# Grouped-query attention: two heads' values in two column groups, as one block at a set place of an explicit TensorE order

## The chip, the cores and the metric

The kernel runs on one core of one Trainium2 chip. The metric is the time of one execution in device microseconds; lower is better. The core has five engines that run side by side: TensorE (PE, its weight loads shown as PEld), VectorE (DVE), ScalarE (ACT), GpSimd (POOL) and SyncE (SP, which here mostly issues transfers), and 16 DMA engines.

## The reference

Two layers of a trunk with two parallel attentions. The change is in branch B, grouped-query attention: 8 query heads of 64 channels share 2 key/value heads. 512 latent tokens look at 768 keys (256 context and 512 latent); in the first layer the 256 context tokens also look at the 256 context keys. All is float32.

```python
def _attend(q, k, v):
    s = jnp.einsum('bqkgd,btkd->bkgqt', q, k).astype(jnp.float32) * (HEAD_DIM ** -0.5)
    p = jax.nn.softmax(s, axis=-1).astype(v.dtype)
    return jnp.einsum('bkgqt,btkd->bqkgd', p, v)

def _merge(a_att, b_att, a_z, b_z, g_a, g_b, w_o_a, w_o_b, w_out):
    o_a = (a_att * jax.nn.silu(a_z)) @ w_o_a
    o_b = (b_att * jax.nn.silu(b_z)) @ w_o_b
    merged = jax.nn.sigmoid(g_a) * o_a + jax.nn.sigmoid(g_b) * o_b
    return merged @ w_out
```

x is 512 x 1024, w_in 1024 x 5376, w_o_a and w_o_b 512 x 1024, w_out 1024 x 1024.

## The kernel before

Each layer projects its input with w_in, runs the neighbourhood attention (branch A), projects branch B's keys, values and queries, runs the grouped-query attention, and then does B's output projection, the merge and the last projection. Float32 accuracy comes from splitting: a projection operand is a high and a low part, and each product is three matmuls (mm3, lines 424 to 426). Probabilities and values are split into two float16 halves each.

**One head of the grouped-query attention, before.** gq_first stages the head's queries (stage_q, lines 872 and 873), all 512 or 768 columns at once. gq_scores goes through four tiles of 128 queries: the scores are four matmuls into one of two PSUM buffers called s (lines 879 and 880); DVE takes the row's maximum (1153); ACT takes the exponential and its sum (1154); turned makes the two float16 halves, the high one by ACT (830), the low one by DVE or, for tiles 1 and 3, by POOL (831); and SP issues a transposing DMA into ht (835). In the first layer ctx_scores does the same for the context queries. gq_values then makes the head's result from ht: divide turns the reciprocal sums by four TensorE transposes (842) and multiplies the gate zb by them (843); then 12 matmuls of 512 columns (1170, 1171) give a PSUM tile whose upper and lower 64 rows belong to the two halves of V; head_out copies one half by ACT (817), adds the other by DVE (818) and lets POOL multiply zb by it (822). ctx_values does the same for the context queries with four matmuls (917).

**Filling.** While DVE, ACT, POOL and the DMAs work on a head, TensorE gets pieces of other projections from a list called fill: the branch gates' columns of w_in that are left (g_chunks, evicted by ACT, 614) and then branch A's output projection (o_chunks, evicted by DVE, 696). One list item is the load of a chunk's weights, or a piece of one feature block and one span of tokens (512 or 256 columns), 24 matmuls for a gate piece and 12 for an output piece; one item, prepare, splits branch A's result into high and low parts (660 by ACT, 661 by POOL). In this stage every piece takes the one PSUM bank called f. The first layer has 40 items left at the first head and the second 24. pipeline runs over the heads: scores of head h, values of head h - 1, then an eighth of the items.

**Order.** The program's order is only a priority: at compile time the framework's scheduler puts each engine's instructions in the order in which it expects them to become ready, and that order is then fixed. behind(engine, fn, after) ties the instructions that fn adds on one engine into a chain behind the named ones; latest(engine, n) names the last n. Before, nothing in the grouped-query attention was tied. Buffers also order: p tiles (NP_GQ, two in the first layer), h tiles (NH_GQ), two ht tiles.

ada_gate finishes the residual gate's modulation: a few DVE instructions, one TensorE transpose (309), an ACT copy, a DMA. In the first layer it stood at the end of the background steps bg, before the attention.

Of the kernel before, what the change touches and what calls it, by code (L numbers as in the profile page):

```python
# [28 lines left out]
NP_GQ = (2, 4)  # L29
# [6 lines left out]
SPLIT_POOL = (1, 3)  # L36
GATES = (3, 3)
PRE_NA, PRE_GQ = 1, 2
ON_PE, ON_DVE = mybir.EngineType.PE, mybir.EngineType.DVE
# [22 lines left out]
def hybrid_kernel(es: ExitStack, tc, x, ctx, cvec, w_ada, w_ada0, small, gvec, w_in, w_o_a, w_o_b, w_out,  # L62
# [521 lines left out]
    def layer(l, hx, nxt, start):  # L584
# [8 lines left out]
        def gate_steps(halves, pool):  # L593
            return (ada_steps(l, range(16, 24), halves, nv, pool)
                    + ([lambda: ada_gate(l, nv, pool)] if 1 in halves else []))
# [128 lines left out]
        else:  # L724
# [5 lines left out]
            bg = gate_steps((0, 1), hp["p"])  # L730
# [49 lines left out]
        if True:  # L780
# [29 lines left out]
            def head_out(po, e, dst, eng=None, back=None):  # L810
# [5 lines left out]
                if back is None:  # L816
                    S.copy(a, po[o:o + 64, :n])
                    V.tensor_tensor(a, po[m:m + 64, :n], a, ALU.add)
                else:
                    S.activation(a, po[o:o + 64, :n], AF.Copy, scale=back[o:o + 64])  # L820
                    V.scalar_tensor_tensor(a, po[m:m + 64, :n], back[m:m + 64], a, ALU.mult, ALU.add)
                (eng or G).tensor_tensor(dst, dst, a, ALU.mult)
# [14 lines left out]
            def divide(ps, r, e, dst, back):  # L837

                n = r.shape[-1]
                V.reciprocal(r, r)  # L840
                for i in range(n):
                    T.transpose(ps[:, 128 * i:128 * i + 128], r[:, i:i + 1].to_broadcast([128, 128]), ident)
                V.scalar_tensor_tensor(dst, ps[64 * e:64 * e + 64, :128 * n], back[64 * e:64 * e + 64], dst,
                                       ALU.mult, ALU.mult)
# [22 lines left out]
            def stage_q(src, e):  # L867

                n = 768 if first else 512
                qs = att["p"].tile([128, n], F32R, tag=f"qs{e}", name=nm("qs"), bufs=1)  # L870
                q = rows(src, e)[:, :n]
# [13 lines left out]
            def ctx_scores(q, kh, kl, ct, late=True):  # L885

                pss = ps_score()
                for i in range(2):
                    scores(pss, q[:, 512 + 128 * i:640 + 128 * i], kh, kl,
                           [(256 * i, 256, cut(512, 768))])  # L890
                mx = sp.tile([128, 2], F32, tag="mx", name=nm("mx"), bufs=8)
                p = p_tile()
                if late:
# [3 lines left out]
                else:  # L897
                    V.tensor_reduce(mx, pss.rearrange("p (i n) -> p i n", i=2), AX, ALU.max, negate=True)
                r = sp.tile([128, 2], F32, tag="r", name=nm("r"), bufs=8)
# [3 lines left out]
                if not late:  # L903
                    softmax_tail(p, 512, r, mx, [(0, 256), (256, 512)])
                turned(p, 512, ct.rearrange("p a i k n -> p (a i k) n"), G)
                return ct, r

            def ctx_values(st, vsl, dst, e, back, late):

                ct, r = st  # L910
                ps = psw(512 if late else 256, "v" if late or not att["spare"] or pm["n"] > 1 else "s")
                po = ps[:, 0:256]
                if late:
                    divide(ps[:, 256:512], r, e, dst, back)
# [4 lines left out]
                head_out(po, e, dst, None, None if late else back)  # L919
# [32 lines left out]
            def na_scores(h, q, kh, kl):  # L952
# [3 lines left out]
                for i in range(4):  # L956
# [25 lines left out]
                    run(att["bg"], 1)  # L982
# [26 lines left out]
            def pipeline(fill, spread, scores_of, values_of, last=None, bg=[]):  # L1009
# [3 lines left out]
                for h in range(8):  # L1013
                    att["bg"] = bg if h > 3 or pm["n"] == 1 else []
# [5 lines left out]
                if last is not None:  # L1020
                    run(fill, len(fill))
                    last()
                run(bg, len(bg))
# [6 lines left out]
            def na_first(h):  # L1030
# [3 lines left out]
                q = stage_q(qav[:, j, :], e)  # L1034
# [5 lines left out]
                return st, ctx_scores(q, kh, kl, ct, False)  # L1040

            def values_of(dst, f, back, late):
                def g(h, st):
                    vsl = f(h, st[0])
                    if first:
                        e = h % 2
                        zv = dst.rearrange("p (f n) -> p f n", f=4)
                        ctx_values(st[1], vsl, zv[64 * e:64 * e + 64, h // 2, 512:768], e, back, late)
                return g

            bg = []
            pipeline(fill, 9, na_first, values_of(za, na_values, vsa[:, 1:2], False), bg=bg)


# [89 lines left out]
            def gq_scores(q, kh, kl):  # L1144
                ht = att["p"].tile([128, 4, 12, 128], F16, tag="ht", name=nm("ht"), bufs=2)
                r = att["p"].tile([128, 4], F32, tag="r4", name=nm("r4"), bufs=3)
                for i in range(4):
                    pss = ps_score(768)
                    scores(pss, q[:, 128 * i:128 * i + 128], kh, kl,
                           [(0, 512, cut(0, 512)), (512, 256, cut(512, 768))])  # L1150
                    p = p_tile()
# [367 lines left out]
```

## Time and profile before

| | us |
|---|---|
| median of three runs | 1107.71 (1105.61 to 1107.86) |
| the profiled execution | 1110.51 |
| its span, first to last instruction | 1108.4 |
| TensorE busy in it | 1073.0 (97%) |
| DVE, ACT, POOL busy | 758.1, 615.1, 470.1 |
| grouped-query attention, first layer | about 381.9 to 545 |
| grouped-query attention, second layer | about 922.4 to 1045 |

In a row of the profile, L1170 is line 1170 of the kernel, the engine and the operation follow, then "out<-in" by the tiles' names, the shapes, and xN for the count. A row of groups ends with the busy time and the mean in ns, then the idle time of the engine just before these instructions and what ended it. A timeline row begins with the start and the duration in us; [1.18 <-DMA ht<-h] at its end is the idle time before it and what released it. A row of waits reads: who waited <- for whom: us in total, times, the longest. A matmul's duration includes its passage through the array, so matmuls that follow each other overlap in the list; what counts is the distance of their starts.

### The profile page before, as it was taken

The numbers are of one execution on the slowest core, as the hardware profiler recorded it, in microseconds if no ns is written. First come the engines' busy times: TensorE is split into PE (matmuls) and PEld (weight loads), VectorE is DVE, ScalarE is ACT, GpSimd is POOL, SyncE is SP. The second block draws the span as 40 slices with busy tenths as digits, with TensorE's granted clock in tenths as the row PEclk, the third lists the DMA queues.
The fourth block names the chain that finished last, engine by engine and source line by source line (L and its number), as shares of the span: only waits on it lengthen the run. The fifth ranks groups of instructions, "written<-read, shape, count | busy, mean of one in ns | idle before, by whom it ended". The sixth has DMA issues, their size and how long they took to land.

```text
span 1108.4 us, 16961 instructions
## 1 busy us (share of the span) xinstructions
PE 1073.0 (97%) x5672; PEld 878.1 (79%) x5672; DVE 758.1 (68%) x1616; ACT 615.1 (55%) x1236; POOL 470.1 (42%) x397
## 2 busy tenths in 40 slices
PE   8999999999999999979899999999999999999998
PEld 5688888788897888767788878888877988777677
DVE  4667789975389467646577795466997665677473
ACT  5455369777342477765331275444999446776420
POOL 1044225554257145454522455232355472564530
PEclk8999999999999999999999999999999999999999
DMA  9355224554544388897643542453565526879642
GB/s 362 146 171 154 86 76 103 137 143 115 169 139 151 100 183 192 176 259 193 160 147 124 171 135 82 136 164 100 133 147 132 164 96 172 207 234 226 187 152 77
DMA packets 236001, 171.79 MB, mean 155 GB/s; under 512 B 160141, under 2 KB 201865, under 8 KB 234249
## 3 DMA queue, kind: packets, MB, share of 16 engines
q1 hardware_dynamic: 228576, 156.31, 51.4%
q0 software_dynamic: 2368, 7.87, 2.2%
q10 hardware_dynamic: 4968, 6.53, 1.9%
q8 instruction: 45, 0.74, 0.3%
q14 instruction: 44, 0.35, 0.1%
HBM read 115.58 MB, written 17.32 MB: 120 GB/s over the span
## 4 chain that ended last, share of the span: by engine, by line
PE 68%; DVE 10%; DMA 6%; issue 6%; ACT 5%; POOL 3%; SPq 1%; POOLq 0%; DVEq 0%; ACTq 0%
PE psx L426 9%; PE psx L425 9%; PE psx L424 9%; PE psf L424 8%; PE psf L425 8%; PE psf L426 8%; PE pss L879 2%; PE pss L880 2%; PE pst L1170 1%; PE pst L1171 1%; PE pst L518 1%; DMA rawb<-in_w_ada_dram 1%; DMA ht<-h 1%; DMA raw<-in_w_in_dram 1%; DVE wlo L411 1%
## 5 line engine op out<-in xcount | busy, mean ns | idle before, releaser
L831 POOL TENSOR_TENSOR h<-p,h 128x256 f16<-128x256 f32 (+2 forms) x104 | 111.7, 1082 | 156.0 <-ACT h L830 108.4
L411 POOL TENSOR_TENSOR wlo<-raw,whi 128x512 fp32r<-128x512 f32 x70 | 96.8, 1387 | 121.4 <-ACT whi L409 90.0
L424 PE MATMUL psf<-hx,whi 128*128 128x512 f32 (+1 forms) x360 | 137.6, 382 | 1.9 <-DVE zt L616 1.2
L426 PE MATMUL psf<-hx,wlo 128*128 128x512 f32 (+1 forms) x360 | 135.4, 376 | 0.0
L425 PE MATMUL psf<-hx,whi 128*128 128x512 f32 (+1 forms) x360 | 135.4, 376 | 0.0
L424 PE MATMUL psx<-whi,hx 128*128 128x512 f32 (+1 forms) x328 | 120.9, 372 | 0.0
L409 ACT CAST whi<-raw 128x512 fp32r<-128x512 f32 x136 | 83.0, 619 | 68.2 <-DMA raw<-in_w_in_dram 47.4
L426 PE MATMUL psx<-whi,hx 128*128 128x512 f32 (+1 forms) x328 | 120.0, 367 | 0.0
L425 PE MATMUL psx<-wlo,hx 128*128 128x512 f32 (+1 forms) x328 | 119.8, 366 | 0.0
L397 POOL TENSOR_TENSOR wlo<-raw,whi 128x512 fp32r<-128x512 f32 x40 | 60.9, 1526 | 118.1 <-ACT whi L394 69.4
L394 ACT CAST whi<-raw 128x512 fp32r<-128x512 f32 x88 | 54.1, 623 | 94.4 <-PE psx L426 38.1
L497 POOL TENSOR_TENSOR ss<-ss,ehalf 128x8 f32<-128x8 f32 (+2 forms) x40 | 64.2, 1609 | 73.7 <-DVE ss L494 68.5
L1153 DVE CUSTOM_DVE_ANT_0 p<-pss,vb 128x768 f32<-128x768 f32 x64 | 60.3, 953 | 43.6 <-PE pss L880 34.5
L830 ACT CAST h<-p 128x256 f16<-128x256 f32 (+2 forms) x136 | 81.6, 616 | 4.2 <-DMA ht<-h 1.4
L411 DVE TENSOR_TENSOR wlo<-raw,whi 128x512 fp32r<-128x512 f32 x66 | 62.7, 952 | 24.5 <-ACT whi L409 23.0
L424 PEld LDWEIGHTS psf<-hx,whi 128*128 128x128 f32 x360 | 67.8, 188 | 14.4 <-DVE zt L616 1.6
L1154 ACT ACTIVATE p<-pss,mx 128x768 f32<-128x768 f32 x64 | 57.6, 901 | 38.4 <-DVE mx L1153 38.2
L426 PEld LDWEIGHTS psf<-hx,wlo 128*128 128x128 f32 x360 | 67.8, 188 | 11.7
L425 PEld LDWEIGHTS psf<-hx,whi 128*128 128x128 f32 x360 | 67.9, 189 | 10.8
L426 PEld LDWEIGHTS psx<-whi,hx 128*128 128x128 f32 x328 | 61.9, 189 | 10.2
L425 PEld LDWEIGHTS psx<-wlo,hx 128*128 128x128 f32 x328 | 62.0, 189 | 9.5
L424 PEld LDWEIGHTS psx<-whi,hx 128*128 128x128 f32 x328 | 61.8, 189 | 9.2 <-issue 0.2
(337 smaller groups left out, 2979.0 us busy)
## 6 DMA issues: line engine op xcount, KB each, us to landing
raw<-in_w_in_dram SPq DMA_DIRECT2D x168, 256.0 KB, 3.0
rawb<-in_w_ada_dram SPq DMA_DIRECT2D x48, 256.0 KB, 2.7
raw<-in_w_out_dram SPq DMA_DIRECT2D x32, 256.0 KB, 2.9
tg<-gs SPq DMA_DIRECT2D x4, 1536.0 KB, 7.1
rawx<-in_w_ada_dram SPq DMA_DIRECT2D x4, 1024.0 KB, 9.8
rawy<-in_w_ada_dram SPq DMA_DIRECT2D x4, 1024.0 KB, 10.8
gs<-zt ACTq DMA_DIRECT2D x16, 256.0 KB, 3.3
raw<-in_w_o_a_dram SPq DMA_DIRECT2D x16, 256.0 KB, 3.1
```

The lines of the kernel that those rows point to most:

```text
L394: S.copy(hi[:, :n], raw[:, :n])
L397: e.tensor_tensor(lo[:, :n], raw[:, :n], F(hi[:, :n]), ALU.subtract)
L409: S.copy(hi, raw)
L411: lo_eng(i).tensor_tensor(lo, raw, F(hi), ALU.subtract)
L424: T.matmul(ps, lhs[0], rhs[0], start=first, stop=False)
L425: T.matmul(ps, lhs[0], rhs[1], start=False, stop=False)
L426: T.matmul(ps, lhs[1], rhs[0], start=False, stop=last)
L497: G.tensor_tensor(ss, ss, ehalf[:, :n], ALU.pow)
L830: S.copy(h[:, 0], p[:, :n])
L831: eng.tensor_tensor(h[:, 1], p[:, :n], h[:, 0], ALU.subtract)
L1153: V.tensor_tensor_reduce(p, pss, lift, -1.0, 3e38, ALU.add, ALU.min, mx[:, 0:1])
L1154: S.activation(p, pss, AF.Exp, bias=mx[:, 0:1], accum_out=r[:, i:i + 1])
```

## The change

- The unit is no longer a head but a pair of heads (j) and half of the queries (b): 8 units a layer, each with two score tiles for each of its two heads. Queries are staged in cuts of 256 columns, the context's apart.
- gq_second makes a unit's result as one block. pair_values takes V's two halves as separate stationary operands of 64 columns; head e writes PSUM rows 64e to 64e + 63, so the two heads of a step stand in two column groups. Three products (high x high, high x low, low x high) add up in PSUM where there were four; 18 steps of two matmuls of 256 columns. The context's block (6 steps) follows for every second unit.
- divide makes the reciprocals wide enough for both heads, so two transposes serve two heads; block and division share a PSUM bank. After the block DVE multiplies once; ACT's copy, the add and POOL's product are gone.
- The block of unit u - 1 stands behind score tile 1 (first layer) or 2 (second layer) of unit u and the filling before it; the filling and scores that come next stand behind the block. The filling is dealt out after every score tile (and the context's), in 40 or 32 parts, where it was dealt out after every head.
- The low halves go to POOL for head 1 of the pair. The first layer has three p tiles. ada_gate moves behind the first unit.

```diff
-NP_GQ = (2, 4)
+NP_GQ = (3, 4)
+VALUES_AT = (1, 2)
...
+            def divide(ps, r, dst, back):
+
+                rb = att["p"].tile([128, 2, 128], F32, tag="rb", name=nm("rb"), bufs=2)
+                V.reciprocal(rb.rearrange("p i (e d) -> p i e d", e=2), r.unsqueeze(3).to_broadcast([128, 2, 2, 64]))
+                for i in range(2):
+                    T.transpose(ps[:, 128 * i:128 * i + 128], rb[:, i, :], ident)
+                V.scalar_tensor_tensor(dst, ps, back, dst, ALU.mult, ALU.mult)
+
+            def pair_values(po, vsl, psl, blocks):
+
+                steps = [(a, q, k) for a, q in ((0, 0), (0, 1), (1, 0)) for k in range(blocks)]
+                for n, (a, q, k) in enumerate(steps):
+                    for e in range(2):
+                        T.matmul(po[64 * e:64 * e + 64].rearrange("p (i n) -> p i n", i=2), vsl(k, q), psl(e, a, k),
+                                 start=n == 0, stop=n == len(steps) - 1)
...
+            def gq_first(u, between):
+
+                j, b = u // 2, u % 2
+                kh, kl = gkt[j // 2]
+                qs = [stage_q(qbv[:, j, :], e, f"qs{e}", 2, 256 * b, 256 * b + 256) for e in range(2)]
...
+                for i in range(2):
+                    for e in range(2):
+                        pss = ps_score(768)
+                        behind(ON_PE, lambda: scores(pss, qs[e][:, 128 * i:128 * i + 128], kh, kl,
+                                                     [(0, 512, cut(0, 512)), (512, 256, cut(512, 768))]), hold)
...
+                        turned(p, 768, ht[:, i, e], G if e == 1 else V)
+                        between(2 * i + e)
...
+            def gq_second(u, st, after):
...
+                for ps, dst, r, _, _, _ in work:
+                    divide(ps[:, 256:512], r, dst, vs[:, 1:2])
+                for ps, dst, _, v, pr, n in work:
+                    behind(ON_PE, lambda: pair_values(ps[:, 0:256], v, pr, n), after)
+                    after = latest(ON_PE, 1)
+                    V.tensor_tensor(dst, ps[:, 0:256], dst, ALU.mult)
...
-            pipeline(fill, 8, gq_first, values_of(zb, gq_values, vs[:, 1:2], True), early)
+            n, parts, prev, filled, hold = len(fill), 8 * (4 + first), [], latest(ON_PE, 1), []
+            for u in range(8):
+
+                def between(t):
+                    nonlocal filled
+                    scored = latest(ON_PE, 1)
+                    hold.clear()
+                    if t == VALUES_AT[l] and prev:
+                        gq_second(u - 1, prev.pop(), scored + filled)
+                        hold.extend(latest(ON_PE, 1))
+                    done = (4 + first) * u + t + 1
+                    behind(ON_PE, lambda: run(fill, len(fill) - (n - n * done // parts)), list(hold))
+                    filled = latest(ON_PE, 1)
+                prev.append(gq_first(u, between))
+                if u == 0 and first:
+                    ada_gate(l, nv, att["p"])
+                if first:
+                    between(4)
+            early()
+            gq_second(7, prev.pop(), filled)
```

More of the change, by code (lines that the diff above doesn't have):

```diff
@@ L593, in gate_steps @@
         def gate_steps(halves, pool):
-            return (ada_steps(l, range(16, 24), halves, nv, pool)
-                    + ([lambda: ada_gate(l, nv, pool)] if 1 in halves else []))
+            return ada_steps(l, range(16, 24), halves, nv, pool)
         gq = gcol[:, 48 + 2 * l:49 + 2 * l]
@@ L865, in stage_k, with stage_q @@
                     S.copy(rows(kl, 1 - e), F(rows(kl, e)))
[L867 to L871, printed above, removed]
+            def stage_q(src, e, tag, bufs, n0, n1):
+                qs = att["p"].tile([128, n1 - n0], F32R, tag=tag, name=nm("qs"), bufs=bufs)
+                q = rows(src, e)[:, n0:n1]
                 S.copy(rows(qs, e), q)
@@ L883, in cut, with ctx_scores @@
                 return lambda k: k[:, a:b]
-            def ctx_scores(q, kh, kl, ct, late=True):
+            def ctx_scores(q, kh, kl, ct, late=None):
                 pss = ps_score()
                 for i in range(2):
-                    scores(pss, q[:, 512 + 128 * i:640 + 128 * i], kh, kl,
-                           [(256 * i, 256, cut(512, 768))])
+                    scores(pss, q[:, 128 * i:128 * i + 128], kh, kl, [(256 * i, 256, cut(512, 768))])
                 mx = sp.tile([128, 2], F32, tag="mx", name=nm("mx"), bufs=8)
                 p = p_tile()
-                if late:
+                if late is None:
+                    r = sp.tile([128, 2], F32, tag="r", name=nm("r"), bufs=8)
+                    V.tensor_reduce(mx, pss.rearrange("p (i n) -> p i n", i=2), AX, ALU.max, negate=True)
+                else:
+                    r = late
                     for i in range(2):
@@ L1007, in na_values, with pipeline @@
                 return vsl
[L1009 removed]
+            def pipeline(fill, spread, scores_of, values_of):
                 n = len(fill)
@@ L1019, in pipeline @@
                     prev = st
[L1020 to L1023, printed above, removed]
                 att["spare"] = True
@@ L1142, in layer @@
             lift = vbig[:, 2950:2951].to_broadcast([128, 768])
[L1144 to L1151, printed above, removed]
-                    mx = sp.tile([128, 2], F32, tag="mx", name=nm("mx"), bufs=8)
-                    V.tensor_tensor_reduce(p, pss, lift, -1.0, 3e38, ALU.add, ALU.min, mx[:, 0:1])
-                    S.activation(p, pss, AF.Exp, bias=mx[:, 0:1], accum_out=r[:, i:i + 1])
-                    turned(p, 768, ht[:, i], G if i in SPLIT_POOL else V)
-                    run(att["bg"], 1)
-                return ht, r
```

108 lines of the change are left out of this document (42 added, 66 removed).

## The prediction

> **What bounds the kernel now.** I read the page's busy times first, then the chain that ended last, then the two stretches in which the grouped-query attention runs (first layer 381.9 to 545 us, second 922.4 to 1045 us), each cut where the gate pieces give way to pieces of the output projection, and last TensorE's waits in them.
>
> ```profile
> PE 1073.0 (97%) x5672; PEld 878.1 (79%) x5672; DVE 758.1 (68%) x1616; ACT 615.1 (55%) x1236; POOL 470.1 (42%) x397
> PE 68%; DVE 10%; DMA 6%; issue 6%; ACT 5%; POOL 3%; SPq 1%; POOLq 0%; DVEq 0%; ACTq 0%
> 381.90:485.00 103.10, 101.36 (x597) 84.38 (x596) 69.27 (x131) 73.87 (x146) 47.05 (x34) 1.00 0.80 172
> 485.00:545.00 60.00, 49.69 (x261) 38.39 (x260) 33.72 (x62) 31.08 (x59) 35.08 (x25) 0.94 0.78 214
> 922.40:985.00 62.60, 61.84 (x298) 48.52 (x297) 40.21 (x66) 47.21 (x86) 29.23 (x20) 1.00 0.73 183
> 985.00:1045.00 60.00, 56.79 (x264) 40.55 (x263) 39.74 (x63) 36.72 (x66) 37.31 (x25) 1.00 0.92 238
> ...
> PE psf L424 <- DVE tg L696: 6.3, 6, 2.5
> PE psf L424 <- ACT zt L614: 3.3, 1, 3.3
> PE pst L1170 <- DMA ht<-h: 1.2, 1, 1.2
> ```
>
> TensorE is the bound: 97% busy, 68% of the chain. In a stretch's row the columns are length, then busy time of PE, PEld, DVE, ACT, POOL, then granted clock, DMA share and GB/s. So TensorE idles 1.7 + 10.3 us in the first layer's attention and 0.8 + 3.2 us in the second's; no other engine passes 76%, but the DMA engines stand at 0.73 to 0.92. In the first layer the idle time is not the values': 9.6 of its 12 us are waits of the filling pieces for their single PSUM bank (the two psf rows), and the values waited for their transposes once, 1.2 us. The clock fell after the long wait:
>
> ```profile
> 480.00:500.00 20.00, 13.56 (x76) 11.53 (x75) 8.30 (x20) 12.22 (x24) 11.79 (x8) 0.86 0.89 298
> 500.00:520.00 20.00, 19.70 (x107) 15.42 (x106) 12.81 (x27) 10.80 (x21) 9.07 (x7) 0.97 0.79 213
> ```
>
> 20 x 0.14 + 20 x 0.03 = 3.4 us of clock lost there. TensorE work taken out of these stretches is thus time gained, if no wait takes its place.
>
> **The values.** Before, a head's block is 12 matmuls of 512 columns (L1170, L1171), the stationary operand holding both halves of V in its 128 columns.
>
> ```profile
> 405.18 0.39 PE L1170 MATMUL pst<-ht,vb 128*128 128x512 f16 x1
> 405.40 0.38 PE L1171 MATMUL pst<-ht,vb 128*128 128x512 f16 x1
> 405.62 0.38 PE L1170 MATMUL pst<-ht,vb 128*128 128x512 f16 x1
> 408.50 0.60 PE L917 MATMUL psv<-vb 128*128 128x256 f16 x4
> 1009.10 0.60 PE L842 MATMUL pst<-ident,r 128*128 128x128 f32 x4
> 18.45 0.60 PE L361 MATMUL pst<-ident,x 128*128 128x128 f32 x4
> 18.98 1.07 PE L243 MATMUL pst<-rawy,scol 128*32 128x256 f32 x16
> 19.98 0.50 PE L1290 MATMUL psx<-whi,hx 128*128 128x512 f32 x1
> L243 PE MATMUL pst<-rawy,scol x16: 379/379/403, 19.0 to 19.7; 128*32 128x256 f32 x16
> L243 PEld LDWEIGHTS pst<-rawy,scol x16: 106/110/110, 19.0 to 19.5; 128*32 128x32 f32 x16
> L1170 PEld LDWEIGHTS <-vb x96: 95/98/100, 405.2 to 1043.2; 128*128 128x128 f16 x96
> ```
>
> Matmuls of 512 columns start 0.216 us apart: 12 x 0.216 = 2.59 us a head. The four of 256 columns in 0.60 us, the last lasting 0.27, are (0.60 - 0.27)/3 = 0.11 apart. After, a unit (two heads, 256 queries) has 18 steps of two matmuls, each 64 columns of weights and 256 moving columns, in two column groups. If the two of a step run side by side, a step is 0.109 us. The kernel already does this once: L243 puts 16 matmuls of 256 columns into four column groups. One after the other they would need at least 16 x 0.11 = 1.7 us; they take 1.07, 0.38 of it the last one's own length, and their 16 loads of 0.11 us fit beneath. Changing between whole array and groups: L1290 starts 0.07 us before L243's end, where within one mode a matmul starts 0.17 before the last one's end (405.40 against 405.18 + 0.39); 0.10 us a change. So a block is 18 x 0.109 + 2 x 0.10 = 2.16 us; there are 8 blocks in each layer, as there were 8 heads: 16 x 0.43 = **-6.9 us**. Bounds for a step: 0.109, and 0.109 + 0.098 = 0.207 if a load of L1170's 0.098 us stood between; I take the lower, since L243 is the nearest row.
>
> Here the Trainium skill speaks against the change: its page "TensorE: Matmul & The Clock Gate", section "Part 3: Packing small matmuls — row/col tiling", says that weight loads overlap running matmuls only where the row groups differ. Both column groups use all rows, so by that rule every step would show its load. L243's row disagrees: its loads also use all rows, and are hidden. That is fp32 with 32 columns, though, not fp16 with 64, so I keep the case as a rival (4): by the rule the sum would be that rival's, by the row it is the one above.
>
> **Context values and divisions.** Context values (first layer): 8 heads x 4 x 0.11 = 3.5 us become 4 pairs x 6 steps x 0.11 = 2.6, in the same block: **-0.9 us**. Divisions: 48 + 32 = 80 transposes of sums (L842, also 0.11 apart by 1009.10) become 24 + 16 = 40: **-4.4 us**.
>
> **The gate's transpose** (ada_gate) leaves the stretch before the attention, where TensorE waited for it, and goes behind the first unit, where scores and fillings stand ahead of it: **-1.8 us**. Its one DMA (L312) now shares SP's queue with the transposing DMAs, a small issue among 40. If the cover fails, the 1.8 us stay.
>
> ```profile
> 371.79 0.27 PE L309 MATMUL pst<-ident,ag 128*16 128x128 f32 x1 [1.84 <-DVE ag L307]
> L817 ACT COPY ho<-pst 64x512 f32<-64x512 f32 x16 | 9.3, 582 | 17.1 <-PE pst L1171 16.9
> L822 POOL TENSOR_TENSOR zb<-zb,ho 64x512 f32<-64x512 f32 (+1 forms) x22 | 27.5, 1250 | 31.2 <-DVE ho L818 24.2 <-DVE r L840 6.5
> 957.70 0.62 ACT L872 CAST qs<-qb 64x512 fp32r<-64x512 f32 x1 [0.81 <-PE pss L880]
> 376.37 1.68 ACT L872 CAST qs<-qb 64x768 fp32r<-64x768 f32 x2
> ```
>
> **Other engines.** Both V halves now add up in PSUM, so L817 leaves ACT (9.3 us and eight smaller copies) and L822 leaves POOL (27.5). Queries are staged in 256-column cuts: by 0.62 us for 512 and 0.84 for 768 columns I estimate 0.42 a cut, so ACT has 40 x 0.42 = 17 us where it had 8 x 0.84 + 8 x 0.62 = 12. ACT, DVE (one product instead of an add) and POOL all end lighter; they are covered by TensorE, so I cost this at nothing. The third p buffer frees DVE's softmax from waiting for POOL. Together TensorE loses 6.9 + 0.9 + 4.4 + 1.8 = **14.0 us**.
>
> **The wait that is added.** Before, nothing tied a values block to a place. Now the block of unit u-1 must follow scores 1 (first layer) or 2 (second) of unit u, and the next filling and the next scores must follow it; the next filling piece is tied too, since all share one PSUM bank. So when the block waits for its last transposed tile, everything on TensorE behind it waits. The tile's way in the second layer:
>
> ```profile
> 957.38 0.28 PE L880 MATMUL pss<-gk,qs 128*128 128x256 f32 x1
> 957.88 0.95 DVE L1153 CUSTOM_DVE_ANT_0 p<-pss,vb 128x768 f32<-128x768 f32 x1
> 959.11 0.89 ACT L1154 ACTIVATE p<-pss,mx 128x768 f32<-128x768 f32 x1
> 959.99 1.56 ACT L830 CAST h<-p 128x768 f16<-128x768 f32 x2
> 961.68 1.67 POOL L831 TENSOR_TENSOR h<-p,h 128x768 f16<-128x768 f32 x1 [5.15 <-PE psf L426]
> ht<-h SPq DMA_TRANSPOSE x144, 3.3
> 378.18 0.39 PE L425 MATMUL psf<-hx,whi 128*128 128x512 f32 x1
> 378.41 0.39 PE L426 MATMUL psf<-hx,wlo 128*128 128x512 f32 x1
> 442.16 0.28 PE L880 MATMUL pss<-gk,qs 128*128 128x256 f32 x1
> 454.93 0.38 PE L1170 MATMUL pst<-ht,vb 128*128 128x512 f16 x1 [1.18 <-DMA ht<-h]
> ```
>
> From the scores' end (957.66) to POOL's end (963.35) 5.7 us, and 3.3 from issue to landing: 9.0 us. The longest shown, in the first layer, is 442.44 to 454.93: 12.5. Against it stands what TensorE has between the last scores of a unit and that unit's block. A filling piece of 512 columns is 24 x 0.23 = 5.5 us in the gate half, half of that for the output projection; four score matmuls are 0.7. Second layer: one gate piece (or two of 2.8) and three scores, 7.6 us, so each block waits 9.0 - 7.6 = 1.4; 7 blocks, 9.8 us. First layer: with gate pieces 5.5 + 2.8 + context scores 0.5 + 1.4 = 10.2, no wait; with output pieces 2.8 + 1.4 + 1.4 + 0.5 + 1.4 = 7.5, 1.5 each for three blocks, 4.5 us. The last block of a layer now stands behind all filling; between its 9.0 us and the next projection's first steps I allow 2 us a layer, 4 in all. Sum **+18.3 us**; bounds: nothing, if the lighter engines bring the way under 7.6, and (12.5 - 7.6) x 7 + (12.5 - 10.2) x 4 + (12.5 - 7.5) x 3 + 4 = 62 us.
>
> **The idle time that goes.** Fillings now come one by one between scores, so a piece finds its bank emptied more often: I take half of the 9.6 us of psf waits (bounds none and all), 2 us of the second layer's 4.0, and the 3.4 us of clock, as no gap of 3.3 us should remain: **-10.2 us**.
>
> **Sum:** -14.0 + 18.3 - 10.2 = **-5.9 us**. The profiled execution took 1110.5 us (span 1108.4 and 2.1 around it), 2.8 over the median of 1107.7. It would come to 1104.6, the median to 1101.8; I say 1101.
>
> **Rivals.** (1) The blocks don't wait: ACT's and POOL's lighter queues shorten the tile's way, and the 18.3 us shrink to 4 or less: -14.0 + 4 - 10.2 = -20, 1087.5 us. For it: L831 on POOL sat idle for ACT's h, and L817's 17.1 us of waiting on ACT for values goes. Against: 7.6 of the 9.0 us are the instructions' and the transfer's own durations (0.95 + 0.89 + 0.78 + 1.67 + 3.3).
> (2) Slower: the wait is longer than 9.0. Each further 0.6 us at 10 blocks is 6 us and eats the gain; at 10.8 us, midway to the 12.5 shown, it is 1.8 x 10 + 0.6 x 4 = +20, with the clock falling again: 1115 to 1122. For it: DMA engines at 0.92 in the second layer's second half. Against: 9 to 10 is the usual length.
> (3) The gains in TensorE's work turn into waits of equal size: 1106 to 1110, the change not doing what it says.
> (4) The groups do not hide their loads, or do not overlap. A step of 0.207 makes a block 3.93, not 2.16: 16 x 1.77 + 24 x 0.098 = +31 us, around 1130; the change stops paying at 1101 + 6.7, which is a step of 0.13. Against it L243's row.
>
> **Numbers.** My forecast's own range, 1095 to 1105.5, has 0.40; rival 1 0.22; rival 3 0.14; rival 2 0.19; rival 4 0.05. A measurement of this kernel can tell about 0.2%, 2.2 us, from no change. Faster 0.62, same 0.14 and slower 0.24. The range 1086 to 1117 takes in rival 1's sum and rival 2's nearer half.
>
> **What the next profile would show.** Two matmuls of a block starting within some 0.01 us of each other and 0.109 us per step proves the groups; 0.2 disproves them. Half the transposes of sums, no L817 copies in the attention. The added wait would appear as values idle for ht's DMA, about 1.4 us a block, most in the second layer. The psf waits for tg and zt should halve, and the clock stay at 1.00 through the first layer's second half. What else would make it wrong: a block shares its PSUM bank with its division, so it also waits for DVE's product; before, context values had that, with 10 us between.

## The result and the profile after

The changed kernel takes 1144.4 us (median of 4 runs, 1142.4 to 1149.0) against 1107.8 us: a ratio of 1.0335, 95% interval 1.0294 to 1.0376. It is 36.6 us slower, where 7 us faster was forecast. In the lengths by stage, taken between the first score matmuls of the two grouped-query attentions and the last matmul's start, the first stretch (first layer's attention, merge and second layer's other attention) grew from 540.5 to 551.9 us, the last (second layer's grouped-query attention and what follows) from 181.5 to 206.0.

The page's busy times and clock row of the changed kernel, and the two attentions cut by stage (length; busy PE, PEld, DVE, ACT, POOL; granted clock, DMA share, GB/s):

```profile
PE 1082.1 (95%) x6032; PEld 896.3 (78%) x6032; DVE 779.8 (68%) x1626; ACT 605.5 (53%) x1236; POOL 436.4 (38%) x375
PEclk9999999999999999989999999999999998899999
381.60:560.00 178.40, 160.30 (x1085) 135.29 (x1084) 114.77 (x194) 99.14 (x203) 65.25 (x43) 0.96 0.73 176
930.00:1100.00 170.00, 146.11 (x828) 119.41 (x827) 104.30 (x158) 89.81 (x165) 61.72 (x40) 0.93 0.67 171
...
922.40:1092.40 170.00, 164.35 (x760) 126.59 (x759) 109.67 (x172) 98.13 (x174) 81.08 (x51) 1.00 0.71 191
```

The last row is the kernel before, over as long a stretch from its second attention on: TensorE idled 170.00 - 164.35 = 5.7 us there, at a clock of 1.00. Now it idles 170.00 - 146.11 = 23.9 us, and the stretch runs at 0.93, which is 170 x 0.07 = 11.9 us more. The clock row (40 slices of 28.6 us) names the place: its two adjacent 8s are 944 to 1001 us. The waits of TensorE in the two stretches (what waited, for what: total, times, longest):

```profile
PE pst L845 <- DVE zb L838: 8.4, 5, 2.6
PE pst L845 <- DMA ht<-h: 6.8, 5, 3.0
PE pss L880 <- ACT p L1150: 4.5, 4, 2.1
PE psf L424 <- DVE tg L695: 2.8, 1, 2.8
...
PE psf L424 <- DVE tg L695: 7.1, 8, 1.5
PE pst L845 <- DMA ht<-h: 5.7, 3, 2.5
PE pst L837 <- DVE rb L835: 2.0, 1, 2.0
```

The upper four are the second layer, the lower three the first. L845 is the paired block: it waited 15.2 us in the second layer, for its transposes (ht) or for its division's product (L838). Before, no values waited in that layer. One unit of the second layer on TensorE's timeline, with DVE and SP beside it (start, length, engine, line; idle time before it in brackets):

```profile
963.18 0.96 DVE L1149 CUSTOM_DVE_ANT_0 p<-pss,vb 128x768 f32<-128x768 f32 x1 [6.81 <-PE pss L881]
967.02 1.66 POOL L826 TENSOR_TENSOR h<-p,h 128x768 f16<-128x768 f32 x1
969.72 1.46 SPq L830 DMA_TRANSPOSE ht<-h  x1
969.77 0.38 PE L837 MATMUL pst<-ident,rb 128*128 128x128 f32 x2
970.57 0.28 PE L881 MATMUL pss<-gk,qs 128*128 128x256 f32 x1
971.71 0.47 DVE L838 SCALAR_TENSOR_TENSOR zb<-pst,vb,zb 128x256 f32<-128x256 f32 x1
972.24 0.27 PE L845 MATMUL pst<-ht,vb 128*64 128x256 f16 x1 [1.39 <-DVE zb L838]
973.65 3.21 PE L845 MATMUL pst<-ht,vb 128*64 128x256 f16 x35 [1.14 <-DMA ht<-h]
...
951.86 4.05 PE L845 MATMUL pst<-ht,vb 128*64 128x256 f16 x36 [2.40 <-DVE zb L838]
1031.51 2.16 PE L845 MATMUL pst<-ht,vb 128*64 128x256 f16 x36
```

The last tile's scores end at about 963.1 (DVE's 963.18 starts on them) and its transposes have landed at 973.65, 10.5 us later. TensorE had work until 970.85, 7.7 us. So it stood 1.39 + 1.14 us, with the next filling and the next scores tied behind the block. The block then ran at a low clock: 35 matmuls in 3.21 us, 36 in 4.05 us after a wait of 2.40, where an undisturbed one takes 2.16.

```profile
970.50:973.50 3.00, 0.62 (x4) 0.25 (x2) 2.97 (x7) 2.92 (x6) 1.07 (x2) 1.00 1.11 295
973.50:977.00 3.50, 3.35 (x36) 2.73 (x37) 0.10 (x2) 1.42 (x3) 1.51 (x1) 0.65 1.12 292
```

So a wait is paid for a second time behind it: 3 us with TensorE busy for 0.62, then 3.5 us at a clock of 0.65. Over the 170 us above it is 11.9 us of clock on 23.9 us of idle time.

### The profile page after: what moved, and what is told of

The parts are those of the page before. It is cut to its first block, busy times and chain, and to the rows that moved or that the text cites. A ratio compares the mean times of both kernels' runs of the same rounds, so it can differ in the third digit from the quotient of the medians.

```text
span 1144.1 us, 17690 instructions
## 1 busy us (share of the span) xinstructions
PE 1082.1 (95%) x6032; PEld 896.3 (78%) x6032; DVE 779.8 (68%) x1626; ACT 605.5 (53%) x1236; POOL 436.4 (38%) x375
## 5 line engine op out<-in xcount | busy, mean ns | idle before, releaser
L411 POOL TENSOR_TENSOR wlo<-raw,whi 128x512 fp32r<-128x512 f32 x70 | 98.2, 1408 | 144.8 <-ACT whi L409 115.5
L397 POOL TENSOR_TENSOR wlo<-raw,whi 128x512 fp32r<-128x512 f32 x40 | 55.8, 1397 | 137.8 <-ACT whi L394 90.0
L426 PEld LDWEIGHTS psf<-hx,wlo 128*128 128x128 f32 x360 | 68.1, 189 | 11.9
## 6 DMA issues: line engine op xcount, KB each, us to landing
rawx<-in_w_ada_dram SPq DMA_DIRECT2D x4, 1024.0 KB, 10.1
```

Of the source, the lines that this page charges most:

```text
L397: e.tensor_tensor(lo[:, :n], raw[:, :n], F(hi[:, :n]), ALU.subtract)
L411: lo_eng(i).tensor_tensor(lo, raw, F(hi), ALU.subtract)
L426: T.matmul(ps, lhs[1], rhs[0], start=False, stop=last)
```

## The experiments

Theory T: the explicit order costs the time, since a wait of the block holds everything on TensorE behind it. Rival R: the paired blocks themselves cost it. All times are medians beside runs of the kernel before on the same chip; "above before" is the difference to those.

| kernel | us | above before | ratio (95%) | first stretch | last |
|---|---|---|---|---|---|
| before | 1107.8 | | | 540.5 | 181.5 |
| after | 1144.4 | +36.6 | 1.0335 (1.0294-1.0376) | 551.9 | 206.0 |
| e1_free | 1115.8 | +6.4 | 1.0058 (1.0038-1.0078) | 544.2 | 181.9 |
| e2_block | 1115.3 | +5.9 | 1.0057 (1.0038-1.0076) | 546.4 | 178.5 |
| e15_tie_block | 1113.6 | +6.0 | 1.0051 (1.0034-1.0068) | 543.6 | 180.4 |
| e21_fill_free | 1127.2 | +18.5 | 1.0162 (1.0128-1.0197) | 549.8 | 184.6 |
| e22_scores_free | 1125.8 | +17.1 | 1.0151 (1.0133-1.0168) | 544.3 | 192.8 |
| e3_later | 1125.9 | +16.5 | 1.0156 (1.0118-1.0193) | 546.1 | 195.2 |
| e4_bank | 1146.1 | +38.5 | 1.0348 (1.0314-1.0382) | 551.3 | 205.2 |
| e18_after_narrow | 1151.9 | +43.3 | 1.0379 (1.0349-1.0409) | 552.6 | 213.0 |
| e10_pin_only | 1163.7 | +54.3 | 1.0510 (1.0463-1.0557) | 561.3 | 215.6 |
| e11_deal_only | 1125.4 | +17.6 | 1.0157 (1.0128-1.0187) | 547.8 | 187.3 |
| e12_free_gate | 1106.3 | -1.4 | 0.9990 (0.9979-1.0000) | 540.4 | 180.9 |
| e17_after_gate | 1141.5 | +33.7 | 1.0309 (1.0279-1.0339) | 549.8 | 205.4 |
| e23_serial | 1125.2 | +17.5 | 1.0154 (1.0125-1.0183) | 553.2 | 188.2 |
| e24_tieb_gate | 1111.0 | +3.2 | 1.0032 (1.0016-1.0049) | 544.4 | 180.6 |
| e16_narrow | 1109.5 | +0.8 | 1.0010 (0.9996-1.0024) | 543.0 | 179.6 |
| e14_before_deal | 1112.0 | +4.4 | 1.0040 (1.0025-1.0056) | 546.3 | 181.1 |
| e28_deal_once | 1110.1 | +1.9 | 1.0015 (0.9995-1.0034) | 543.0 | 180.5 |
| e29_before_order | 1105.8 | -2.4 | 0.9980 (0.9959-1.0001) | 538.3 | 180.5 |

The two right columns are stage lengths of the one profiled execution of each, as above.

**Is it the ties?** e1_free drops all three from the changed kernel:

```diff
-  behind(ON_PE, lambda: scores(pss, ...), hold)
+  scores(pss, ...)
-  behind(ON_PE, lambda: pair_values(ps[:, 0:256], v, pr, n), after)
+  pair_values(ps[:, 0:256], v, pr, n)
-  behind(ON_PE, lambda: run(fill, ...), list(hold))
+  run(fill, ...)
```

> The changed kernel (paired column-group blocks, divisions of 128x128 transposes, the filling dealt out after each tile) with no order tied on TensorE: scores, values and filling are sent as the scheduler likes. Theory T (the set place costs the time: the block waits for its transposes and the division's product with all TensorE work held behind it, and the clock halves behind each such wait): the waits in front of L845 and L838 (about 28 us in the two attentions of after) and the half-clock stretches (12 us) go, the shorter TensorE work (11 us) stays: 1107.8 - 11 = 1097 us, between 1090 and 1106. Rival R (the paired blocks and the rest of the new units cost it: 64-column loads, changes of mode, rows of 256 staged): nothing of that goes with the ties, 1135 to 1150 us.

30 of the 36.6 us go with the ties, and the last stretch is back to 181.9: rival R falls. But theory T's 1097 was also missed by 19 us: more than the ties is lost. Which tie is it? e2_block keeps a block's 36 matmuls in one piece at no set place (`behind(..., [])`); e15_tie_block keeps the block's tie to its place and frees scores and filling; e21_fill_free frees the filling alone, e22_scores_free the scores alone. Each edits the same three calls.

> As the kernel without ties, but the 36 matmuls of a paired block are chained one behind the other, at no set place. Theory T: the place costs, not that the block is one piece; within 4 us of the kernel without ties, about 1097 us (1090 to 1108), with blocks of 2.16 us. Rival B (the block as one piece costs: what is ready on TensorE can't slip between its matmuls while one of them waits for a late transpose): over half of the loss of the changed kernel is back, 1120 to 1145 us. Rival R: 1135 to 1150 us.

> The changed kernel with one of the ties alone: the paired block stands behind the scores and the filling dealt out so far, but what comes after it (scores, filling) is not held behind it, and neither are scores and filling tied among themselves. Theory T (it is the work held behind the block that pays for its wait): the scheduler puts scores and filling in front of a block that isn't ready, and the time is that of the kernel without ties, 1110 to 1122 us. Rival P (the block's place itself costs, since TensorE takes its instructions in order): 1130 to 1146 us.

> The changed kernel with the filling alone untied; scores and the paired blocks keep their order. The block tied alone cost nothing (1113.6 against 1115.8 us without ties), so the 28.6 us are in what else is tied. Theory F (the filling behind the block is what would cover its wait, and chained filling stops for its own PSUM bank, 9.8 us of waits for tg, with scores behind it): nearly all comes back, 1112 to 1122 us. Rival S (the scores tied behind the block start every tile's softmax late): 1134 to 1146 us. Rival both: in between.

> The changed kernel with the scores alone untied; the filling is tied behind the scores and blocks before it, the blocks at their place. Theory F (the tied filling is the cost): little comes back, 1132 to 1146 us. Rival S (the scores tied behind the block are): 1112 to 1124 us, since the next tile's scores can cover the block's wait and start early.

Neither that the block is one piece nor its tie to a place costs anything here (+5.9, +6.0 against +6.4; for the tie, e24_tieb_gate below says otherwise). What costs is what is held behind it, and that is shared: freeing the filling gives 18 us, freeing the scores 19.5, so that both runs fall between their two theories. By stage they differ: freeing the filling gives 21.4 us in the last stretch and 2.1 in the first, freeing the scores 13.2 and 7.6. TensorE's waits in the second layer with the filling free:

```profile
PE pst L845 <- DMA ht<-h: 1.9, 1, 1.9
PE pss L880 <- ACT p L1150: 1.5, 2, 0.9
PE pst L845 <- DVE zb L838: 1.3, 1, 1.3
```

The block now waits 3.2 us there, not 15.2, with the scores still tied: that fits filling standing in front of it while it isn't ready.

**Would a later place, or an earlier product, have done?** e3_later moves the block; e4_bank gives the division its own PSUM tile.

```diff
-VALUES_AT = (1, 2)
+VALUES_AT = (4, 3)
-  if t == VALUES_AT[l] and prev:  gq_second(u - 1, prev.pop(), ...)
+  if t == VALUES_AT[l] and u:     gq_second(u - 1, prev.pop(0), ...)
```
```diff
-  divide(ps[:, 256:512], r, dst, vs[:, 1:2])
+  divide(psw(256, "t"), r, dst, vs[:, 1:2])
```

> The changed kernel with the block set later: behind the context scores in the first layer (place 4 in place of 1) and behind the last tile in the second (3 in place of 2). A tile of the second layer is 4.1 us of TensorE work, in the first the place moves by some 16 us. Theory T: the waits in front of the block were 1.1 to 3.0 us each with 10.7 us from scores' end to landing, so one tile more covers them all; the waits for transposes and products (about 28 us with the score waits behind them) and the clock's 12 us go except at the last unit of each layer: 1105 us, between 1096 and 1118. Rival R: the place is not what costs, 1136 to 1150 us. Rival S (whatever is tied waits: the scores and filling behind it too, at any place): 1118 to 1136 us.

> The changed kernel with the division of a block in a PSUM tile of its own, so that the block no longer shares a bank with it and needn't wait for the product of L838. In the changed kernel PE waited 9.2 us for that product, 6 times, and 12.5 us for transposes, 8 times. Theory T (the transposes land last anyway): where the product released the block, its second matmul waited some 1.1 us more for ht; a block that starts without the product waits for ht instead, and little is gained: 1138 to 1146 us. Rival B (the shared bank is the cost): the 9.2 us and the half clock behind those waits, some 6 us, go: 1124 to 1133 us.

The later place gives 20 of the 36.6 us: rival S. In the second layer the block's waits for ht shrink to 3.3 us, but the scores tied behind it now wait for the softmax (first row below). The own bank gives nothing. The waits for the product are gone from its second layer, and those for the transposes are nearly as long as both were together (13.8 us against 15.2; last row): the transposes land last anyway.

```profile
PE pss L880 <- ACT p L1150: 6.9, 3, 3.3
PE pst L845 <- DMA ht<-h: 3.3, 2, 2.3
...
PE pst L845 <- DMA ht<-h: 13.8, 7, 4.8
```

**What are the paired blocks worth?** e10_pin_only is the kernel before with the new order around its own values; e11_deal_only is that without the ties, so that the dealing per tile and the earlier place of the values in the program are left; e12_free_gate and e17_after_gate are e1_free and the changed kernel with ada_gate put back at the end of `gate_steps`. e23_serial is e12_free_gate with the loops of a block exchanged.

```diff
 # e10: in the kernel before
+  behind(ON_PE, lambda: scores(...), hold)        # each tile's scores
+  behind(ON_PE, block, after)                     # the 12 matmuls of a head's values
+  behind(ON_PE, lambda: run(fill, ...), list(hold))  # a share after each tile
 # e11: the same places, without behind()
 # e12, e17
-  if u == 0 and first: ada_gate(l, nv, att["p"])
+  ada_steps(...) + ([lambda: ada_gate(l, nv, pool)] if 1 in halves else [])
 # e23
-  for n, (a, q, k) in enumerate(steps):
-      for e in range(2):
+  for e in range(2):
+      for n, (a, q, k) in enumerate(steps):
```

> The kernel before (one head's values over 128 rows, four transposes a division, no column groups) with the explicit order alone: scores, filling dealt out after each tile, and the values block of the head before at the same places as in the changed kernel. Theory T: the set place costs it without any paired block; waits of about 28 us and half-clock stretches of about 12 us on top of 1107.8: 1148 us, between 1128 and 1165. Rival R (the paired blocks cost it): the order costs nothing, 1100 to 1112 us.

> The kernel before (values of one head over 128 rows, nothing tied, ada_gate as it was) with the filling dealt out after each tile, and the values of the head before behind the second or third tile, instead of all behind the head's four tiles. Theory D (the dealing is worth some us by itself: with paired blocks the kernel that deals once a unit stood at 1112.0, the one that deals per tile at 1106.3): 1107.7 - 5 = 1103 us, between 1098 and 1105.5. Rival E (it is worth nothing with one head's values): 1106 to 1110 us. With theory D the paired blocks themselves would have given 1106 - 1103, a loss of 3 us; with E a gain of 1.5.

> The kernel without ties, with ada_gate put back to where the kernel before has it (at the end of the gate's steps, ahead of the attention). Without ties PE waited 4.6 us at 364 us in front of the attention (L518 for DVE's rr), where the kernel before waited 1.8 us for ag. Theory G (ada_gate's move lets rr fall behind the late products of L286, and costs the difference): 1115.8 - 3 = 1113 us, between 1110 and 1114.5. Rival N (it is the weights' DMA that is late, and whatever is next waits for it): no change, 1114.5 to 1118 us.

> The changed kernel, all ties kept, with ada_gate put back ahead of the attention. Without ties that gave 9.5 us, of which 3.7 in front of the attention and 4 in the first layer's attention and merge. Theory A (the two add up): 1144.4 - 9.5 = 1135 us, between 1131 and 1138. Rival M (only the wait in front goes, 3.7 against 1.8 us, with its half clock; the rest is taken up by the tied block's waits): 1139 to 1144 us.

> The kernel without ties and with ada_gate ahead of the attention (1106.25 us), whose blocks do all matmuls of one head and then all of the other, so that no two column groups stand side by side. A pair of matmuls started every 0.109 us in a block of 2.16 us; one behind the other at the same pace a block takes 36 x 0.109 = 3.9 us and one of context values 12 x 0.109 = 1.3 us. Theory G (the side-by-side groups are worth what their matmuls say, TensorE being the bound): 16 x 1.76 + 4 x 0.65 = 31 us more, 1137 us, between 1130 and 1143. Rival W (waits take back what TensorE is spared, and would also give way to more of its work): half or less of that, 1108 to 1121 us.

Line numbers in these kernels are a little shifted: a block is L846 in e12 and e23, a head's values L1179 and L1180 in e10.

With ada_gate in its old place, four kernels make a square (us above before; the filling dealt per tile in all four):

| | nothing tied | scores, values, filling tied |
|---|---|---|
| values of one head | e11: +17.6 | e10: +54.3 |
| paired blocks | e12: -1.4 | e17: +33.7 |

The ties cost 36.7 and 35.1 us, the paired blocks give 19.0 and 20.6: the two add up, and theory T holds in both rows. The lower row holds all of the new units (paired blocks, wide divisions, a third p tile, other staging), and its gain is one over kernels that deal per tile; how it stands with the filling dealt as before is tried below. From e12 to e17 only the ties change. The pages' busy times (e12 above, e17 below), and e17's largest waits:

```profile
PE 1067.9 (97%) x6032; PEld 883.3 (80%) x6032; DVE 783.8 (71%) x1626; ACT 607.3 (55%) x1236; POOL 443.3 (40%) x375
PE 1078.8 (95%) x6032; PEld 894.2 (79%) x6032; DVE 779.9 (68%) x1626; ACT 605.7 (53%) x1236; POOL 442.0 (39%) x375
PE pst L846 <- DMA ht<-h: 10.9, 9, 2.7
PE psf L424 <- DVE tg L696: 10.1, 9, 2.7
```

The profiled executions' spans are 1105.7 and 1138.7 us. Of the 33.0 us between them, 22.1 are idle time of TensorE (37.8 to 59.9), and 10.9 are the same 6032 matmuls taking longer, at a granted clock of 0.982 over the span where it was 0.996. e10's largest wait in the second layer, without any paired block, is again the values' for their transposes:

```profile
PE pst L1179 <- DMA ht<-h: 17.2, 6, 4.7
```

e11 missed both its theories: I expected the dealing to gain or to do nothing, and with one head's values it costs 17.6 us, together with the values' earlier place. Its trace shows waits of the filling for zt and one wait of a division that the kernel before doesn't have (rows below); they weren't taken apart.

```profile
PE pst L843 <- DVE r L841: 6.4, 1, 6.4
PE psf L425 <- ACT zt L615: 6.3, 4, 2.7
```

e12 gave more than its theory said (7.8 against 3), e17 only 2.9, which its interval does not tell from nothing: of ada_gate's move some 3 us are the wait in front of the attention, which both had (after: L518, below), and the rest in e12 lies in the first layer's attention, where a new order of the untied matmuls came with it.

```profile
367.71 1.09 PE L518 MATMUL pst<-ident,rr 128*128 128x128 f32 x4 [3.66 <-DVE rr L575]
PE pst L309 <- DVE ag L307: 1.7, 1, 1.7
```

The first row is the changed kernel's; in e12 it is gone, and the second, ada_gate's own wait, is there again. e23_serial shows the groups' own worth. The second layer's blocks in groups of instructions, e12_free_gate above and e23_serial below (busy, mean ns):

```profile
L846 PE MATMUL pst<-ht,vb 128*64 128x256 f16 x288 | 17.8, 274 | 0.0
L846 PE MATMUL pst<-ht,vb 128*64 128x256 f16 x288 | 31.9, 282 | 0.0
```

That is 17.8 / 8 = 2.2 us a block side by side and 31.9 / 8 = 4.0 one after the other. TensorE was busy for 1093.6 us in e23's profiled execution, 25.7 more than in e12's, where 31 were reckoned; 19 arrive at the end: between theory G's and rival W's ranges. The Trainium skill's rule weighed in the prediction (page "TensorE: Matmul & The Clock Gate", section "Part 3: Packing small matmuls — row/col tiling": loads overlap running matmuls only where row groups differ) does not hold here as it stands: both column groups use all rows, and 36 loads fit beneath 2.2 us. What hides them, no run here shows.

**Does DVE eat the gain?** The division's reciprocal now runs over 128x256, and I had called DVE lighter. e16_narrow is e12_free_gate with it over 128x4 again; e18_after_narrow is the changed kernel with the same edit. e24_tieb_gate is e15_tie_block with ada_gate back.

```diff
-  V.reciprocal(rb.rearrange(...), r.unsqueeze(3).to_broadcast([128, 2, 2, 64]))
+  V.reciprocal(r, r)
+  G.tensor_copy(rb.rearrange(...), r.unsqueeze(3).to_broadcast([128, 2, 2, 64]))
```

> The kernel without ties and with ada_gate ahead of the attention (1106.25 us), with the division's reciprocal taken over the 128x4 sums, as before the change, and spread to the 128x256 operand of the two transposes by a copy on POOL. L836, the reciprocal of 128x256, took DVE 1.75 us, 20 times (35 us); before it was 128x4 or 128x2 in 0.17 us, 24 times (4 us). Theory D (31 us more on DVE, which also takes the softmax's first step, is what ate the column groups' gain: PE waited 6.9 us for ACT's p and 2.6 us for rb): those waits fall back to the 0.9 us of before and the time to 1106 - 7 = 1099 us, between 1094 and 1103. Rival N (TensorE covers what DVE does): 1104.5 to 1108 us.

> The changed kernel, ties and all, with the same narrow reciprocal and POOL's copy. Theory D: the product L838 that the tied block waited for (9.2 us in 6 waits) comes some 1.2 us earlier, and tiles' softmaxes too, so that waits of all kinds shrink: 1128 to 1138 us. Rival L (ht lands last in any case, as an own bank showed): 1140 to 1148 us.

> The paired block tied behind the scores and the filling so far, nothing else tied, and ada_gate ahead of the attention. Theory A (the block's tie costs nothing, as with ada_gate late, 1113.6 against 1115.8 us): 1113.6 - 9.5 = 1104 us, between 1102 and 1107.5. Rival M (the two overlap): 1108 to 1113 us.

Theory D falls. The reciprocal went from 1.75 us (below, the changed kernel's) to 0.17, DVE's busy time from 783.8 to 751.5 us, and the time did not fall: 1.4 us below before, then 0.8 above; with ties it was +43.3 against +36.6. TensorE's waits for the softmax went from 6.9 us to 4.5 (4.2 below and one of 0.3), not to the 0.9 of before (below the reciprocal's row: the kernel before, then e12_free_gate, then e16_narrow):

```profile
L835 DVE RECIPROCAL rb<-r x16: 1746/1750/1753, 394.4 to 1069.0; 128x256 f32<-128x256 f32 x16
PE pss L879 <- ACT p L1154: 0.9, 2, 0.5
...
PE pss L881 <- ACT p L1151: 5.2, 6, 1.5
PE pst L838 <- DVE rb L836: 2.6, 2, 1.4
PE pst L846 <- DMA ht<-h: 2.0, 3, 0.9
PE pss L881 <- ACT p L903: 1.7, 2, 1.1
...
PE pss L882 <- ACT p L1152: 4.2, 4, 1.8
PE pst L847 <- DMA ht<-h: 3.6, 1, 3.6
```

e24_tieb_gate came out at +3.2, rival M. Against e12_free_gate (-1.4), which has the same place of ada_gate and no tie, the block's tie alone cost 4.6 us, and the two intervals lie apart: that the tie is free held only with ada_gate late.

**Can the paired blocks beat the kernel before?** e14_before_deal is e12_free_gate with the own bank of e4_bank and the filling dealt once a unit; e28_deal_once has the dealing alone; e29_before_order also puts the values behind all of a unit's scores, as in the kernel before.

```diff
 # e14, e28: in between(t)
-  run(fill, len(fill) - (n - n * done // parts))
 # behind a unit's scores
+  run(fill, len(fill) - (n - n * (u + 1) // 8))
 # e29 also (with the lines of e3_later for prev)
-VALUES_AT = (1, 2)
+VALUES_AT = (4, 3)
```

> The kernel without ties with three things as before the change: the division in a PSUM tile of its own, ada_gate ahead of the attention, and the filling dealt out once a unit, behind its scores and the values of the unit before. What is left of the change are the paired blocks, the wide divisions and the units of 256 rows of two heads. Theory C (the column groups save 11 us of TensorE work, and waits made by these three things ate it in the kernel without ties): 1107.8 - 11 + 3 = 1100 us, between 1095 and 1106. Rival U (the units themselves lose it: their scores wait for the softmax, L880 4.3 us and 1.2 us without ties against 0.9 us before, and DVE has 25 us more to do): 1107 to 1116 us.

> The kernel without ties and with ada_gate ahead of the attention (1106.25 us), with the filling dealt out once a unit, behind its scores, as before the change; the division shares its bank with the block. Theory B (the bank of its own, not the dealing, cost the kernel that had both 6 us; dealing per tile cost the kernel before 17.6 us): 1106.25 - 6 = 1100 us, between 1094 and 1104. Rival D (paired units want the filling per tile): 1109 to 1115 us.

> As the kernel that deals once a unit, with the values of the unit before behind all scores of the unit, as in the kernel before the change. Of the change are left the paired blocks, the wide divisions and the units of two heads. Theory C (with before's order the 14 us that TensorE is spared come through as they did between paired and serial blocks, 19 of 31): 1107.8 - 14 x 0.6 = 1099 us, between 1095 and 1104. Rival U (units of two heads and their divisions lose it): 1106 to 1114 us.

e14 and e28 are not faster than before (rivals U and D, e28's interval taking in no change). Dealt once a unit, as before the change, the new units thus give nothing: the 19 us of the square are a gain over e11, not over the kernel before. e29 is 0.998 of before, interval 0.9959 to 1.0001: between its two theories, at best 4 us better, and not told from no change. No kernel here beats the one before by more than the measurement can tell.

## Why the prediction was wrong, by its steps

Going from the kernel before by way of e12 and e17 to the changed one, the 36.6 us are: the new units with nothing tied -1.4, the ties +35.1, ada_gate's place +2.9. The prediction's sum had, for the same three, -22.4 (-12.2 for the TensorE work without the gate and -10.2 for the idle time that the dealing should save), +18.3 and -1.8. Two steps failed: the gains that didn't come, 21 us, and the price of the tied order, 17 us too low. By way of e11 and e10 the same total reads dealing +17.6, ties +36.7, paired blocks -20.6, ada_gate +2.9. The ties cost as much on both ways; the first and the third term belong to that way alone, since with paired units the kernel that deals once a unit (e28) was not faster than the one that deals per tile (e12), but 3.3 us slower.

- **Column groups and divisions: right in kind, their worth too large (-12.2); this is part of the first step that failed.** The two groups do run side by side, about 0.11 us a step ((2.16 - 0.27) / 17), and the transposes of sums fell from 80 to 40. That a block's row reads 2.16 us, the digits forecast, is luck: the row runs to the end of the last matmul, while the forecast counted starts and two changes. Counted like the forecast, from the last matmul in front of a block to the second behind it (before in the first two rows, e12 in the last two):

```profile
1013.59 0.28 PE L880 MATMUL pss<-gk,qs 128*128 128x256 f32 x1
1016.54 0.39 PE L425 MATMUL psf<-gal,whi 128*128 128x512 f32 x1
1014.02 0.28 PE L882 MATMUL pss<-gk,qs 128*128 128x256 f32 x1
1016.65 0.40 PE L882 MATMUL pss<-gk,qs 128*128 128x512 f32 x1
```

These are 2.95 and 2.63 us. Less 0.12 and 0.23 for the two matmuls beside it, a block cost 2.60 us before and 2.28 now: 0.32 saved, not 0.43, as the two changes take 2.28 - 18 x 0.109 = 0.32 us and not 0.20. Over all, TensorE's busy time fell by 5.1 us (1073.0 to 1067.9 in e12), not 12.2, and some 2 of them are a higher clock (0.996 against 0.994 over the span). The rest of the difference was not taken apart.

- **The idle time that goes (-10.2): the other part of that step.** With nothing tied the filling's waits for tg do fall, as forecast (rows below: before, then e12). But waits for the softmax rise from 0.9 to 6.9 us and 2.6 us for rb come in, rows above, and TensorE's idle time in the profiled execution goes from 35.4 to 37.8 us. That is rival 3, gains that turn into waits, and its 1106 to 1110 us is about where e12, e28 and e29 stand (1106.3, 1110.1, 1105.8). With the ties the waits for tg are back as well: 10.1 us in e17.

```profile
PE psf L424 <- DVE tg L696: 7.2, 8, 2.5
PE psf L424 <- DVE tg L696: 1.8, 2, 1.0
```

- **The added wait (+18.3): right in kind and place, its price too small by half; this is the second step that failed.** In the unit shown the slack was sized well (7.7 us measured, 7.6 forecast). The tile's way was not: 10.5 us for 9.0. Up to POOL's end it took 5.6 us, as forecast (5.7), but SP issued the transpose 1.0 us after that (968.68 to 969.72), and the transfer took 3.9 us for 3.3. That unit's wait was 2.5 us for 1.4. The block also waited for its division's product, which the prediction named as a risk but gave no price; that one hides under the transposes (e4_bank). All waits of the blocks in the changed kernel, 12.5 us for ht and 9.2 for the product, are not far above the 18.3 forecast. What the sum lacked is the rest that the ties bring: the other tied work's waits, tg's above all, and the clock. Rival 2 had the longer way, and with 10.8 us it priced it at 1115 to 1122; it too left out most of the rest:
- **The clock, inside the same step.** The prediction had the clock stay at 1.00, as no gap of 3.3 us should remain. That reads its own trace wrongly: before, the clock stayed at 1.00 behind the wait of 3.34 us and fell at one of 2.46 (rows in the last section), and the changed kernel's blocks have waits of 2.4 to 3.0 us in front of them. By the windows' rows the clock cost 178.4 x 0.04 = 7.1 us in the first layer's attention, where as long a stretch before had lost 3.6, and 11.9 in the second's, where before had lost none.
- **ada_gate (-1.8): wrong.** The wait that stood in front of ada_gate's transpose now stands in front of L518's (3.66 us): the next transpose waits for DVE instead. Putting ada_gate back gave 7.8 us with nothing tied and 2.9 with the ties, the latter not told from nothing. Why DVE is late there was read only from the trace (its products L286 wait for the weights' DMA) and not tried.
- **DVE lighter, at no cost: wrong premise, right price.** 20 reciprocals of 1.75 us are 35 us, where 24 of 0.17 were 4. Taking them out changed nothing for the better.

What stays open: why TensorE waits longer for the softmax in the new units. DVE's load is not all of it: without 32 us of that load the waits were 4.5 us, and the time was no shorter. Between paired and serial blocks 19 of 25.7 us of TensorE's busy time came through, three quarters; by that the 5.1 us of e12 would give 3.8, where 1.4 were measured, with an interval from 0 to 2.3. Why the dealing costs 17.6 us with one head's values is open too. Untied kernels also differ by 2 to 8 us from one edit to the next, so the single steps among them (e12, e24, e28, e14) are not priced closer than their intervals.

## What to carry to other kernels

An explicit order on an engine is priced by what is held behind the instruction that may wait: leave the work that could cover it free to go in front. Take the slack and the way of the late operand both from the trace, then add what the clock loses behind the waits, here 11.9 us on 23.9 us of idle time. And a saving on the engine that bounds the kernel should be tried alone before an order is built around it: here -22.4 us of forecast gains came to -1.4 without any order (e12), and an order that cost 35 us hid with them behind one sum of -6.

## What the runs showed of the hardware that was not expected

TensorE's clock does not go by the length of the last gap alone. In the kernel before:

```profile
489.11 0.50 PE L424 MATMUL psf<-gah,whi 128*128 128x512 f32 x1 [3.34 <-ACT zt L614]
495.55 0.58 PE L424 MATMUL psf<-gah,whi 128*128 128x256 f32 x1 [2.46 <-DVE tg L696]
489.10:493.10 4.00, 3.33 (x12) 2.10 (x12) 0.00 (x0) 0.47 (x1) 4.00 (x3) 1.00 0.97 380
495.50:501.00 5.50, 5.45 (x20) 4.97 (x21) 3.12 (x6) 2.61 (x6) 0.00 (x0) 0.50 1.08 229
```

Behind the wait of 3.34 us the granted clock was 1.00 for 4 us; behind the one of 2.46 it was 0.50 for 5.5. In the changed kernel a block took 4.05 us after 2.40 us of waiting, and after 1.39 + 1.14 us with one matmul between, 35 matmuls took 3.21, at a granted clock of 0.65 over 3.5 us. In e12 it was 0.50 from 479.30 to 482.70, behind 3.40 us in which TensorE was busy for 1.61 and no wait was longer than 1.38. The Trainium skill's page "TensorE: Matmul & The Clock Gate", section "Part 1: The HAM clock gate", lets the clock fall after an idle window of about 3.4 us; here it fell with shorter gaps, and with TensorE busy for 0.62 of 3.00 us or 1.61 of 3.40. DVE's reciprocal of 128x256 took 1.75 us where its products of the same shape (L838) took 0.47.
